# GpSimd out of all operand splits, Silu on ScalarE in half of the heads, and a new order of projections and next weights in a two-block layer stack

## The chip, the core and the metric

The kernel runs on one core of a Trainium2 chip. The metric is the device time of one execution in microseconds (us), the median of several runs. A core has five engines that run side by side, each in its own order: TensorE (PE) multiplies, VectorE (DVE) does elementwise work, ScalarE (ACT) applies functions and copies, GpSimd (POOL) does slower elementwise work and some data movement, SyncE (SP) issues most DMAs. They wait for each other through semaphores.

## The reference, cut to what matters

`reference()` runs 256 tokens of width 1024 through two blocks. The first has a state-space mixer, a stick-breaking attention and two feed-forward layers (FFN, inner width 2816) with RMS norms. The second block has two layers of the form FFN, hybrid mixer, FFN, each followed by a layernorm of residual plus update. The hybrid mixer is what the change is mostly about:

```python
def hybrid_mixer(x, w_in, conv_w, ...):
    hcat = x @ w_in                       # one wide projection, split into:
    qa, ka, va, qkv_b, beta_raw, dt_raw, z, gate_raw = jnp.split(hcat, SPLIT_POINTS, axis=-1)
    ya = sliding_window_attention(qa, ka, va, pos_bias, sink) @ w_branch_a
    qkv_b = jax.nn.silu(causal_depthwise_conv(qkv_b, conv_w))      # width 4, 3072 channels
    qb, kb, vb = jnp.split(qkv_b, (QK_B, 2 * QK_B), axis=-1)
    qb, kb = l2norm(qb), l2norm(kb)       # per head of 128: t * rsqrt(sum(t*t) + 1e-6)
    ...
    o = gated_delta_rule(qb, kb, vb, g, beta)     # chunked recurrence, 8 heads
    yb = (rmsnorm(o) * dn_norm_g * silu(z)) @ w_branch_b
    return (sigmoid(gate_a) * ya + sigmoid(gate_b) * yb) @ w_out
```

## The kernel before, in words

**Operands in two parts.** Matmuls are done in a fast float32 form whose operands are first split: `split` (L151) lets ScalarE copy a tile into the high part `h` (L153), and then the low part is `l = src - h` (L157). Each product is three matmuls (`mm3`: high x low, high x high, low x high). With `share`, the last `share` columns of the subtract are done by GpSimd, the rest by DVE. Only the 48 units of the convolved projections (24 per mixer) use a share, `SH_C = 512` of 1024 columns.

**Weight units.** `unit` (L161) loads 512 KB (128 x 1024) through SP into one of three `raw` buffers and splits it into `wh` and `wl`. The raw buffer is free again when both have read it. `behind_norm` orders a unit's split behind the instructions that stand in `c.norm`: the last ones of a norm, or of the splits of its transposed output.

**Order.** `weave` writes PE's order by hand. It steps through the fill list (projections, one after another) and through lanes (the small chains: heads, windows, prep), which yield how much PE work must pass, or the name of something that has to be done, before they go on. The other engines' order is made by a planner from dependences, priorities and its own estimate of time; a norm with its transposes (`urgent`) has precedence.

**Ends of stages.** `last_rows` (L281) ends a row-wise matmul stage. It keeps the last units' weights and does the first 128 tokens (t = 0) with all of them, starts that half's norm (`tail`), then does t = 1 with its own norm. Before all of that it calls `early`, which loads and splits the first four units of the next stage. The norm's output is transposed on PE, and split (`xx`), 3.9 us of planned PE work after the tail's start; the next stage's products of t = 0 come then, and behind them the transposes of t = 1. There are nine such ends with a next stage: four with an RMS norm, three FFN ends with a layernorm, two ends of `w_out` (five kept units in place of six) with a layernorm.

**The hybrid mixer's projections.** Its fill list is `z_first()`, `betas()`, `conv_half(0)`, `conv_half(1)`, `qkv_a()`, `z_gate(2)`, `z_gate(3)`, the gates, and branch a. `conv_half(f)` does four heads: four keys (n = 1), four queries (n = 0), then four values (n = 2), each a `conv` (L1150): 24 matmuls, then the last tap on ScalarE (L1157), three taps on DVE (L1081, 255, 254 and 253 columns), a Tanh on ScalarE, and a closing product on DVE, `(tanh(a/2) + 1) * a`, twice the silu. `qkv_a` does the windowed attention's two key units, one value unit pair and eight query units, without a convolution. A window lane starts when its query is done.

**prep.** `prep(f)` (L1312) waits until all keys and queries of its half are there, squares them on ScalarE (L1320), sums the squares by four matmuls with `sel` on PE, and goes on to the decay rows, a round trip through DRAM, the Gram matrices of four heads and a small triangular inverse on GpSimd. Heads of that half wait for it.

Of the kernel before, what the change touches and what calls it, by code (L numbers as in the profile page):

```python
# [1 line left out]

# [14 lines left out]
T = 256  # L17
# [74 lines left out]
class Core:  # L92
# [68 lines left out]
    def unit(self, src, share=0, hold=False, stay=False):  # L161
# [11 lines left out]
        with self.behind_norm():  # L173
            self.split(h, l, raw, share)
# [69 lines left out]
    def toks256_steps(self, out, src, x, share=0):  # L244
        ws = [self.unit(src[j], share) for j in range(2)]
        for t in range(2):
            yield from self.toks(out, ws, x, t)
# [45 lines left out]
    def row_gemm(self, units, g, tail, hold=None, wait=lambda j: None, apart=True, share=0):  # L293
# [5 lines left out]
        for j in range(n):  # L299
# [4 lines left out]
            w = self.unit(units[j], share, apart and j >= n - hold)  # L304
# [208 lines left out]
PS = ()  # L513
# [10 lines left out]
def ssm(c, yT, after):  # L524
# [27 lines left out]
    with ExitStack() as ctx:  # L552
# [233 lines left out]
        def group(kt):  # L786
# [94 lines left out]
            c.split(yT[0][:, kt, :], yT[1][:, kt, :], y, 256 if kt in PS else 0)  # L881
# [179 lines left out]
ORD = 2  # L1061
# [8 lines left out]
SH_C = 512  # L1070
# [3 lines left out]
def hybrid(c, i, hT, state, place):  # L1074
# [11 lines left out]
    with ExitStack() as ctx:  # L1086
# [56 lines left out]
        def beta_cols():  # L1143
            for f in range(2):
# [3 lines left out]
                V.tensor_copy(out=bcol[:, f], in_=pt)  # L1148

        def conv(f, n, m):  # L1150

            src = n * NH + m
            w = c.unit(W("qkv")[src], SH_C)
# [26 lines left out]
        def conv_half(f):  # L1180
            heads = range(f * NHH, f * NHH + NHH)
            for n in (1, 0):
                for m in heads:
                    yield from conv(f, n, m)
            c.done.add(f"kq{f}")
            if f == 0:
                beta_cols()
            for m in heads:
                vT[m] = yield from conv(f, 2, m)
                c.done.add(f"vT{m}")  # L1190
# [7 lines left out]
        def qkv_a():  # L1198
            for m in range(2):
                ka[m] = keep1(T)  # L1200
                yield from plain(W("ka")[m], ka[m], 1.0)
# [4 lines left out]
            for m in range(KD):  # L1206
                qa[m] = keep1(T)
                yield from plain(W("qa")[m], qa[m], 0.125)
                c.done.add(f"qa{m}")
# [327 lines left out]

        weave(c,
# [356 lines left out]
```

## Time and profile before

| | |
|---|---|
| median of 3 runs | 2198.07 us (2197.18 to 2202.41) |
| the profiled execution's own time | 2201.57 us |
| its span, first to last instruction | 2199.7 us |
| mean granted TensorE clock | 0.984 of full speed |
| PE busy | 2120.7 us, 96% of the span |
| DVE busy | 1535.2 us, 70% |
| ACT busy | 1181.9 us, 54% |
| POOL busy | 227.4 us, 10%; 77.1 us of it in 48 half subtracts |
| chain that ended last | PE 68%, DVE 11%, DMA 8%, issue 5%, ACT 4%, POOL 2% |

The page gives each engine's busy time, the span in 40 slices, the chain of work that ended last, and groups of instructions by line, tile and shape with their mean duration and the idle time before them. The matmuls are pipelined, so a busy PE may still be late; what tells is how many matmuls a stretch holds, where PE waits and for whom, and where the granted clock is 0.5 (the 1.2 GHz level) instead of 1 (2.4 GHz). The two mixers lie between 906 and 1245 us and between 1642 and 1980 us.

### The profile page before, as it was taken

The numbers are of one execution on the slowest core, as the hardware profiler recorded it, in microseconds if no ns is written. First come the engines' busy times: TensorE is split into PE (matmuls) and PEld (weight loads), VectorE is DVE, ScalarE is ACT, GpSimd is POOL, SyncE is SP. The second block draws the span as 40 slices with busy tenths as digits, with TensorE's granted clock in tenths as the row PEclk, the third lists the DMA queues.
The fourth block names the chain that finished last, engine by engine and source line by source line (L and its number), as shares of the span: only waits on it lengthen the run. The fifth ranks groups of instructions, "written<-read, shape, count | busy, mean of one in ns | idle before, by whom it ended". The sixth has DMA issues, their size and how long they took to land.

```text
span 2199.7 us, 36566 instructions
## 1 busy us (share of the span) xinstructions
PE 2120.7 (96%) x13908; PEld 1855.6 (84%) x13908; DVE 1535.2 (70%) x2615; ACT 1181.9 (54%) x2187; POOL 227.4 (10%) x360
## 2 busy tenths in 40 slices
PE   8799999999999999998999999999999899999998
PEld 7677888898888888887899888888889688998886
DVE  8855777675877666788755776676678876576665
ACT  4644656444655555465655455545546565544553
POOL 1001000000000000342400000000005242000000
PEclk9889999999999999999999999999999999999999
DMA  4315576534666565554433655556555453355663
GB/s 145 104 38 171 184 249 200 174 117 131 199 188 210 174 190 192 169 173 141 140 100 115 219 172 191 185 192 191 189 181 166 138 169 107 103 183 185 193 190 123
DMA packets 123471, 362.02 MB, mean 165 GB/s; under 512 B 24732, under 2 KB 38000, under 8 KB 123296
## 3 DMA queue, kind: packets, MB, share of 16 engines
q1 hardware_dynamic: 117696, 350.25, 51.1%
q0 software_dynamic: 5232, 9.37, 1.5%
q8 instruction: 110, 1.80, 0.3%
q14 instruction: 65, 0.53, 0.1%
q10 hardware_dynamic: 368, 0.07, 0.0%
HBM read 355.36 MB, written 5.04 MB: 164 GB/s over the span
## 4 chain that ended last, share of the span: by engine, by line
PE 68%; DVE 11%; DMA 8%; issue 5%; ACT 4%; POOL 2%; SPq 0%; POOLq 0%; ACTq 0%; DVEq 0%
PE ps L37 65%; DVE wl L157 4%; PE ps L41 3%; ACT wh L153 3%; DMA raw<-in_ffn_w_dram 3%; DVE keep L1081 1%; DVE k L1081 1%; DMA raw<-in_w_out_dram 1%; DMA raw<-in_ffn_w_down_dram 1%; DMA k<-scratch 1%; DMA raw<-in_w_in_z_dram 1%; DMA raw<-in_ssm_w_glu_dram 1%; DMA raw<-in_w_in_qkv_dram 1%; DVE prod L536 1%; POOL u L1080 0%
## 5 line engine op out<-in xcount | busy, mean ns | idle before, releaser
L37 PE MATMUL ps<-xx,wh 128*128 128x256 f32 (+1 forms) x4064 | 1065.5, 337 | 4.9 <-DVE xx L157 2.1
L157 DVE TENSOR_TENSOR wl<-raw,wh 128x1024 fp32r<-128x1024 f32 (+1 forms) x614 | 737.1, 1203 | 321.1 <-ACT wh L153 310.4
L153 ACT CAST wh<-raw 128x1024 fp32r<-128x1024 f32 x614 | 643.4, 1050 | 314.5 <-PE ps L37 157.5
L37 PE MATMUL ps<-xx,wl 128*128 128x256 f32 x2992 | 798.2, 280 | 0.5 <-DVE wl L157 0.5
L37 PEld LDWEIGHTS ps<-xx,wh 128*128 128x128 f32 x4064 | 678.6, 189 | 91.0 <-issue 18.9
L37 PEld LDWEIGHTS ps<-xx,wl 128*128 128x128 f32 x2992 | 563.7, 188 | 21.4 <-DVE wl L157 0.9
L37 PE MATMUL ps<-wh,xx 128*128 128x256 f32 (+1 forms) x1152 | 256.0, 317 | 0.8 <-DVE xx L157 0.7
L230 ACT COPY sum<-ps 128x256 f32<-128x256 f32 x240 | 88.7, 371 | 247.2 <-PE ps L37 246.9
L37 PE MATMUL ps<-wl,gh 128*128 128x512 f32 x528 | 208.9, 396 | 0.0
L37 PE MATMUL ps<-wh,gl 128*128 128x512 f32 x528 | 208.6, 395 | 0.2 <-DVE gl L157 0.2
L37 PE MATMUL ps<-wh,gh 128*128 128x512 f32 x528 | 208.3, 394 | 0.0
L37 PEld LDWEIGHTS ps<-wh,xx 128*128 128x128 f32 x1152 | 190.8, 190 | 17.0 <-DVE xx L157 2.6
L37 PE MATMUL ps<-wl,xx 128*128 128x256 f32 (+1 forms) x576 | 187.7, 326 | 3.8 <-DVE wl L157 3.8
L231 DVE TENSOR_TENSOR sum<-ps,sum 128x256 f32<-128x256 f32 x240 | 101.0, 422 | 108.6 <-ACT sum L230 108.4
L37 PEld LDWEIGHTS ps<-wl,xx 128*128 128x128 f32 x576 | 109.7, 190 | 13.4 <-issue 2.8
L37 PEld LDWEIGHTS ps<-wh,gl 128*128 128x128 f32 x528 | 99.1, 188 | 24.0 <-DVE gl L157 0.9
L37 PEld LDWEIGHTS ps<-wh,gh 128*128 128x128 f32 x528 | 99.3, 188 | 23.3
L37 PEld LDWEIGHTS ps<-wl,gh 128*128 128x128 f32 x528 | 99.2, 188 | 19.1
L337 POOL TENSOR_SCALAR v<-mv 128x1 f32<-128x1 f32 x12 | 7.3, 610 | 846.4 <-DVE mv L394 846.4
L153 ACT CAST xx<-ps 128x512 fp32r<-128x512 f32 (+1 forms) x64 | 31.8, 512 | 107.0 <-PE ps L41 106.5
L157 POOL TENSOR_TENSOR wl<-raw,wh 128x512 fp32r<-128x512 f32 x48 | 77.1, 1613 | 69.6 <-ACT wh L153 64.3
L1081 DVE SCALAR_TENSOR_TENSOR k<-ps,cw,k 128x255 f32<-128x255 f32 x144 | 68.4, 475 | 2.2
(291 smaller groups left out, 2315.0 us busy)
## 6 DMA issues: line engine op xcount, KB each, us to landing
raw<-in_ffn_w_dram SPq DMA_DIRECT2D x264, 512.0 KB, 3.6
raw<-in_ffn_w_up_dram SPq DMA_DIRECT2D x88, 512.0 KB, 3.6
raw<-in_w_in_qkv_dram SPq DMA_DIRECT2D x48, 512.0 KB, 3.7
raw<-in_ffn_w_down_dram SPq DMA_DIRECT2D x44, 512.0 KB, 3.5
raw<-in_w_in_gate_dram SPq DMA_DIRECT2D x32, 512.0 KB, 3.6
raw<-in_w_branch_dram SPq DMA_DIRECT2D x32, 512.0 KB, 3.5
raw<-in_ssm_w_glu_dram SPq DMA_DIRECT2D x16, 512.0 KB, 4.0
raw<-in_w_in_z_dram SPq DMA_DIRECT2D x16, 512.0 KB, 4.3
```

The source lines that it names most:

```text
L37: self.pe.matmul(out, lhsT=lhsT, rhs=rhs, start=start, stop=stop)
L41: self.pe.transpose(out, in_, ident)
L153: o = [self.nc.scalar.copy(out=h, in_=src).ins]
L157: r = e.tensor_tensor(out=l[..., c], in0=src[..., c], in1=h.bitcast(F32)[..., c], op=ALU.subtract)
L230: self.nc.scalar.copy(out=s, in_=ps[:, 1])
L231: self.nc.vector.tensor_tensor(out=s, in0=ps[:, 0], in1=s, op=ALU.add)
L337: nc.gpsimd.tensor_scalar(out=v, in0=ms, scalar1=scale, scalar2=eps, op0=ALU.mult, op1=ALU.add)
L536: e.tensor_tensor(out=o, in0=a, in1=b, op=op)
L1081: stt = lambda o, a, s, b, op0, op1, e=V: e.scalar_tensor_tensor(out=o, in0=a, scalar=s, in1=b, op0=op0, op1=op1)
```

## The change

GpSimd's share goes from every split. `split` gets a flag `behind`, and only the DVE subtract of a unit, no longer ScalarE's copy, is ordered behind `c.norm`. In the first four heads, keys and queries of the convolution take one Silu on ScalarE in place of a Tanh and a product; since they are no longer doubled, the epsilon of their norm changes with them. `prep` waits for one query after another, squares each pair of key and query behind its query, and sums them as they come. The convolutions of the second four heads alternate with the attention's keys, values and queries. And `last_rows` calls `early` after the tail of t = 0 has been started.

```diff
-    def split(self, h, l, src, share=0):
-        o = [self.nc.scalar.copy(out=h, in_=src).ins]
-        n = src.shape[-1] - share
-        for e, c in ((self.nc.vector, slice(0, n)), (self.nc.gpsimd, slice(n, None))):
-            if c.start != src.shape[-1] and c.stop != 0:
-                r = e.tensor_tensor(out=l[..., c], in0=src[..., c], in1=h.bitcast(F32)[..., c], op=ALU.subtract)
-                o.append(r.ins)
-        return o
+    def split(self, h, l, src, behind=False):
+        o = self.nc.scalar.copy(out=h, in_=src)
+        with self.behind_norm() if behind else ExitStack():
+            r = self.nc.vector.tensor_tensor(out=l, in0=src, in1=h.bitcast(F32), op=ALU.subtract)
+        return [o.ins, r.ins]
@@ unit
-        with self.behind_norm():
-            self.split(h, l, raw, share)
+        self.split(h, l, raw, True)
@@ last_rows
-        if self.early:
-            self.early()
-            self.early = None
         for t in range(2):
             for n in range(2):
                 for w, g, first in held:
                     self.rows(acc, w, t, g, first, w is held[-1][0], (n,))
                     yield 1
             self.start(tail(t, acc[2 * t:2 * t + 2]))
+            if self.early:
+                self.early()
+                self.early = None
@@ conv (24 per mixer)
-            w = c.unit(W("qkv")[src], SH_C)
+            w = c.unit(W("qkv")[src])
...
-            h = k1(T)
-            c.act(out=h, in_=a, func=AF.Tanh, scale=0.5)
-            if n == 2:
-                stt(h, h, 1.0, a, ALU.add, ALU.mult)
-                return h
             if n == 1:
                 kq[m] = keep2(2, T)
-            stt(kq[m][:, 1 - n], h, 1.0, a, ALU.add, ALU.mult)
+            if n < 2 and f == 0:
+                c.act(out=kq[m][:, 1 - n], in_=a, func=AF.Silu)
+            else:
+                h = k1(T)
+                c.act(out=h, in_=a, func=AF.Tanh, scale=0.5)
+                stt(h if n == 2 else kq[m][:, 1 - n], h, 1.0, a, ALU.add, ALU.mult)
+            if n == 0:
+                c.done.add(f"q{m}")
+            if n == 2:
+                vT[m] = h
+                c.done.add(f"vT{m}")
@@ prep
-            yield f"kq{f}"
-            pss = c.ps(2, T)
-            sq = []
+            pss = None
             for h in range(NHH):
-                sq.append(k2(2, T))
-                S.activation(out=sq[h], in_=kq[f * NHH + h], func=AF.Square)
-            yield hop()
-            for h in range(NHH):
-                PE.matmul(pss[:NHH], lhsT=sel[:, h, :], rhs=sq[h], start=h == 0, stop=h == NHH - 1)
-                yield 0.4
+                yield f"q{f * NHH + h}"
+                yield hop()
+                sq = k2(2, T)
+                S.activation(out=sq, in_=kq[f * NHH + h], func=AF.Square)
+                yield hop()
+                if h == 0:
+                    pss = c.ps(2, T)
+                PE.matmul(pss[:NHH], lhsT=sel[:, h, :], rhs=sq, start=h == 0, stop=h == NHH - 1)
+            yield 0.8
             lr = k2(2, T, part=NHH)
-            V.tensor_scalar(out=lr, in0=pss[:NHH], scalar1=4e-6, scalar2=None, op0=ALU.add)
+            V.tensor_scalar(out=lr, in0=pss[:NHH], scalar1=(EPS, 4 * EPS)[f], scalar2=None, op0=ALU.add)
@@ the mixer's fill list
+        (kq0, v0), (kq1, v1) = conv_half(0), conv_half(1)
+        light = [keys_a(0), keys_a(1), values_a()] + [queries(m) for m in range(KD)]
+        mixed = [g for pair in zip_longest(kq1 + v1, light) for g in pair if g]
...
-               2: [z_first(), betas(), conv_half(0), conv_half(1), qkv_a(), z_gate(2), z_gate(3),
-               gates(0, ca), gates(1, gb), branch_a()],
+              [z_first(), betas(), *kq0, beta_cols(), *v0, *mixed, z_gate(2), z_gate(3), gates(0, ca), gates(1, gb),
+               branch_a()])
@@ attention to FFN (first block)
-        def early():
-            ho.append(c.pair(1))
-            ho.extend(up_ahead(ho[0], 1))
-            c.early()
         def to_ffn(t, acc):
+            if t == 0:
+                ho.append(c.pair(1))
+                ho.extend(up_ahead(ho[0], 1))
             yield from to_norm(ho[0], g)(t, c.add(t, acc))
```

## Rows read from the trace of the kernel before

**Rows 1.** The page, first part: busy us, share of the span, instructions.
```profile
PE 2120.7 (96%) x13908; PEld 1855.6 (84%) x13908; DVE 1535.2 (70%) x2615; ACT 1181.9 (54%) x2187; POOL 227.4 (10%) x360
```
**Rows 2.** Stretches: length, busy us (instructions) of PE, PEld, DVE, ACT, POOL; clock; DMA.
```profile
925.00:950.00 25.00, 25.00 (x216) 24.85 (x215) 22.11 (x39) 17.41 (x31) 13.85 (x11) 1.00 0.66 208
1000.00:1025.00 25.00, 19.50 (x112) 13.98 (x111) 21.74 (x53) 14.61 (x28) 0.00 (x0) 0.86 0.26 90
1250.00:1275.00 25.00, 21.05 (x108) 17.86 (x107) 16.40 (x24) 4.32 (x5) 3.38 (x4) 0.86 0.55 184
1725.00:1750.00 25.00, 16.98 (x93) 11.76 (x92) 20.77 (x46) 13.20 (x27) 5.19 (x3) 0.86 0.42 130
```
**Rows 3.** PE's waits, whole span: us in total, times, longest us.
```profile
PE ps L37 <- ACT k L1320: 11.7, 7, 4.5
PE ps L41 <- DVE x L399: 11.2, 5, 4.2
```
**Rows 4.** PE's waits from 975 to 1025 us, the same columns.
```profile
PE ps L37 <- ACT k L1320: 5.5, 3, 4.5
PE ps L37 <- DVE keep L1080: 1.1, 1, 1.1
```
**Rows 5.** DVE's groups by shape, whole span: busy us, mean ns, idle before.
```profile
L157 DVE TENSOR_TENSOR wl<-raw,wh 128x1024 fp32r<-128x1024 f32 x566 | 692.4, 1225 | 313.8 <-ACT wh L153 303.4 <-PE ps L41 1.3
...
L157 DVE TENSOR_TENSOR wl<-raw,wh 128x512 fp32r<-128x512 f32 x48 | 44.9, 935 | 7.2 <-ACT wh L153 6.9
L157 DVE TENSOR_TENSOR xx<-ps,xx 128x512 fp32r<-128x512 f32 x40 | 27.2, 688 | 26.6 <-ACT xx L153 26.6
L1081 DVE SCALAR_TENSOR_TENSOR keep<-k,k 128x256 f32<-128x256 f32 x32 | 24.3, 760 | 4.3 <-ACT k L279 4.2
...
L1081 DVE SCALAR_TENSOR_TENSOR k<-k,k 128x256 f32<-128x256 f32 x16 | 10.0, 625 | 2.7 <-ACT k L279 2.7
```
**Rows 6.** DVE in order of time, convolutions: start, us, line, operation, tiles, shape.
```profile
935.06 1.53 DVE L1081 SCALAR_TENSOR_TENSOR keep<-k,k 128x256 f32<-128x256 f32 x1
...
939.19 0.41 DVE L1081 SCALAR_TENSOR_TENSOR keep<-k,k 128x256 f32<-128x256 f32 x1
```
**Rows 7.** ACT's groups by shape from 922 to 1000 us.
```profile
L279 ACT ACT_TABLE_LOAD x2 | 2.6, 1283 | 0.0
```
**Rows 8.** ACT's groups by shape, whole span: the FFN's Silu.
```profile
L415 ACT ACTIVATE s<-sum 128x256 f32<-128x256 f32 x80 | 33.4, 417 | 1.3 <-DVE sum L231 1.2
```
**Rows 9.** PE in order of time, first w_out end; idle before in brackets.
```profile
1259.32 0.39 PE L37 MATMUL ps<-wl,xx 128*128 128x512 f32 x1
1259.55 0.62 PE L37 MATMUL ps<-wh,xx 128*128 128x512 f32 x2
1264.11 1.11 PE L41 MATMUL ps<-ident,x 128*128 128x128 f32 x4 [3.94 <-DVE x L399]
```
**Rows 10.** DVE in order of time at the same place.
```profile
1257.36 2.48 DVE L157 TENSOR_TENSOR wl<-raw,wh 128x1024 fp32r<-128x1024 f32 x2 [1.69 <-ACT wh L153]
1259.75 0.69 DVE L391 SCALAR_TENSOR_TENSOR xn<-ps,x 128x512 f32<-128x512 f32 x1
1260.47 0.69 DVE L392 BATCH_NORM_STATS2 st<-xn 128x6 f32<-128x512 f32 x1
...
1263.30 0.75 DVE L399 SCALAR_TENSOR_TENSOR x<-xn,r,gain 128x512 f32<-128x512 f32 x1 [0.45 <-POOL r L339]
```
**Rows 11.** DVE in order of time, an FFN's end.
```profile
1449.06 0.67 DVE L391 SCALAR_TENSOR_TENSOR xn<-ps,x 128x512 f32<-128x512 f32 x1
...
1452.10 1.40 DVE L399 SCALAR_TENSOR_TENSOR x<-xn,r,gain 128x512 f32<-128x512 f32 x2
```
**Rows 12.** PE at the same FFN's end, second transposes.
```profile
1462.34 0.60 PE L41 MATMUL ps<-ident,x 128*128 128x128 f32 x4
```
**Rows 13.** The page, DMA issues: queue, count, KB each, us to landing.
```profile
raw<-in_ffn_w_dram SPq DMA_DIRECT2D x264, 512.0 KB, 3.6
```

More of the change, by code (lines that the diff above doesn't have):

```diff
@@ L1 @@
 from contextlib import ExitStack
+from itertools import zip_longest
 import numpy as np
@@ L148, in norm_pools, with unit @@
         self.gain = self.pool(ctx, "gain", 2)
-    def split(self, h, l, src, share=0):
-        o = [self.nc.scalar.copy(out=h, in_=src).ins]
-        n = src.shape[-1] - share
-        for e, c in ((self.nc.vector, slice(0, n)), (self.nc.gpsimd, slice(n, None))):
-            if c.start != src.shape[-1] and c.stop != 0:
-                r = e.tensor_tensor(out=l[..., c], in0=src[..., c], in1=h.bitcast(F32)[..., c], op=ALU.subtract)
-                o.append(r.ins)
-        return o
-    def unit(self, src, share=0, hold=False, stay=False):
+    def split(self, h, l, src, behind=False):
[3 more added lines that the diff above has]
+        return [o.ins, r.ins]
+    def unit(self, src, hold=False, stay=False):
         raw = (self.hold_raw if hold else self.raw).tile([P, 1024], F32, name="raw")
@@ L242, in toks, with toks256_steps @@
                 yield 1
-    def toks256_steps(self, out, src, x, share=0):
-        ws = [self.unit(src[j], share) for j in range(2)]
+    def toks256_steps(self, out, src, x):
+        ws = [self.unit(src[j]) for j in range(2)]
         for t in range(2):
@@ L291, in last_rows, with row_gemm @@
             self.start(tail(t, acc[2 * t:2 * t + 2]))
-    def row_gemm(self, units, g, tail, hold=None, wait=lambda j: None, apart=True, share=0):
+            if self.early:
+                self.early()
+                self.early = None
+    def row_gemm(self, units, g, tail, hold=None, wait=lambda j: None, apart=True):
         n, held, acc, hold = units.shape[0], [], None, hold or HOLD
@@ L303, in row_gemm @@
                 acc = [self.ps() for _ in range(4)]
-            w = self.unit(units[j], share, apart and j >= n - hold)
+            w = self.unit(units[j], apart and j >= n - hold)
             if j < n - hold:
@@ L512 @@
 NR = 2
-PS = ()
 TURNS = {0: (0,), 1: (1,), 3: (2,), 5: (3,)}
@@ L880, in group @@
             S.activation(out=y, in_=y, func=AF.Gelu_apprx_tanh)
-            c.split(yT[0][:, kt, :], yT[1][:, kt, :], y, 256 if kt in PS else 0)
+            c.split(yT[0][:, kt, :], yT[1][:, kt, :], y)
             c.done.add(f"y{kt}")
@@ L1060 @@
 QQ = (2, 2)
-ORD = 2
 VF = 14.0
@@ L1069 @@
 LW = 2
-SH_C = 512
 HOP = 2.4
@@ L1148, in beta_cols @@
                 V.tensor_copy(out=bcol[:, f], in_=pt)
+            yield 0
         def conv(f, n, m):
             src = n * NH + m
-            w = c.unit(W("qkv")[src], SH_C)
+            w = c.unit(W("qkv")[src])
             p = c.ps(T)
@@ L1181, in conv_half @@
             heads = range(f * NHH, f * NHH + NHH)
[L1182 to L1190, printed above, removed]
+            return [conv(f, n, m) for n in (1, 0) for m in heads], [conv(f, 2, m) for m in heads]
         def plain(src, dst, scale):
@@ L1196, in plain, with queries, keys_a, values_a @@
             S.activation(out=dst, in_=p, func=AF.Copy, scale=scale)
[L1198 to L1201, printed above, removed]
+        def queries(m):
+            qa[m] = keep1(T)
+            yield from plain(W("qa")[m], qa[m], 0.125)
+            c.done.add(f"qa{m}")
+        def keys_a(m):
+            ka[m] = keep1(T)
+            yield from plain(W("ka")[m], ka[m], 1.0)
+        def values_a():
             p = c.ps(2, T)
@@ L1205, in qkv_a @@
             S.copy(out=ka["v"], in_=p)
[L1206 to L1209, printed above, removed]
         def z_first():
@@ L1543, in hybrid @@
                ] + [[window(j) for j in range(n, KD, LW)] for n in range(LW)],
-              {0: [z_first(), betas(), conv_half(0), qkv_a(), conv_half(1), z_gate(2), z_gate(3),
-               gates(0, ca), gates(1, gb), branch_a()],
-               1: [betas(), conv_half(0), z_first(), conv_half(1), qkv_a(), z_gate(2), z_gate(3),
-               gates(0, ca), gates(1, gb), branch_a()],
-               2: [z_first(), betas(), conv_half(0), conv_half(1), qkv_a(), z_gate(2), z_gate(3),
-               gates(0, ca), gates(1, gb), branch_a()],
-               3: [z_first(), betas(), conv_half(0), z_gate(2), z_gate(3), conv_half(1), qkv_a(),
-               gates(0, ca), gates(1, gb), branch_a()],
-               4: [z_first(), betas(), conv_half(0), gates(0, ca), conv_half(1), qkv_a(), z_gate(2), z_gate(3),
-               gates(1, gb), branch_a()]}[ORD])
+              [z_first(), betas(), *kq0, beta_cols(), *v0, *mixed, z_gate(2), z_gate(3), gates(0, ca), gates(1, gb),
+               branch_a()])
         cT = c.pair(place)
@@ L1743, in first_block @@
         out = c.row_gemm(I["attn_w_o"], c.ktiles(oT), to_ffn, 4, wait=lambda j: f"o{max(j, 5)}")
-        c.early = early
         stick_breaking(c, hk, state, 1, c.gains(I["norm_mix"][1]), oT, [out, go()])
```

## The prediction

> **What bounds the kernel now.** I read the busy shares, then TensorE (PE) in stretches, then PE's waits, and then the engine that each wait names. PE is busy for 96% of the span, so time is to be won only where PE stands still or runs on the slow clock [rows 1]. In the dense stretch 925:950 PE issues 216 matmuls; in 1000:1025 it issues 112, in 1725:1750 only 93, and in both the granted clock is 0.86, that is some 7 us at the 1.2 GHz level (0.14 x 25 x 2) [rows 2]. Both are the same place of the two hybrid mixers: the projections with the causal convolution are just over. Of all PE's waits the longest are on the squares of prep (11.7 us) and on the layernorm's output (11.2 us) [rows 3]. The squares are waited for because VectorE (DVE) is behind: it is busy 22.1 of 25 us in the convolutions, against 25 us of a PE that never stops there [rows 2], and the ScalarE squares can't start before DVE's last product of the convolution.
>
> **Why DVE is behind.** In the 48 convolution units GpSimd subtracts columns 512 to 1023. That leaves DVE 935 ns for its half; a whole 1024 columns takes 1225 ns [rows 5]. And the closing product takes 1.53 us in one unit and 0.41 us in a later one [rows 6]; its mean is 760 ns for q and k (32 of them) and 625 ns for v (16) [rows 5]. In the slow one a GpSimd subtract runs beside it. So the half given away saves DVE little and costs it elsewhere.
>
> **Part 1, split and silu.** DVE loses 44.9 us of half subtracts and gains 48 x 1.225 = 58.8 us. Of the 32 products of q and k, 16 become one Silu on ScalarE: 16 x 0.76 = 12.2 us less. The other 16 and the 16 of v fall to 0.41 us: 16 x 0.35 + 16 x 0.215 = 9.0 us less. Sum: -7.3 us of DVE, 3.7 per mixer. On ScalarE a Silu of this shape takes 417 ns [rows 8] and replaces a Tanh of the same shape; the Silu's own function table adds two loads per mixer (in, and back to Tanh and Exp), 4 x 1.28 = 5.1 us [rows 7], beside 7.6 us of idle ScalarE in 25 us [rows 2]: I cost them at nothing; if that cover failed, +5.1.
>
> **Part 2, the order.** So far 24 convolution units stand in a row. Now 12 do, and the other 12 alternate with 11 plain units (attention queries, keys, values), each of which asks DVE only for the 1.2 us subtract. DVE per convolution unit was 0.94 + three taps + 0.76; it is now 1.23 + three taps + 0.41 or 0, and the second half of the units is spread over twice the PE time. What this can remove: the 11.7 us of waits on squares, 1.1 us of a neighbouring wait in each mixer of which I take half [rows 4], and the slow clock that follows the stop. PE works through about 4.8 of those 7 us and loses half of that, 2.4 per mixer. Sum: 11.7 + 1.1 + 4.8 = 17.6 us.
> What comes back: the squares now follow each query and may not be late by more than two hops of PE work. In the second half they fall into prep(0)'s own DVE work, and the window lanes, whose queries come earlier, bring theirs into the same stretch. The nearest row for such a wait is the one removed, 4.5 us [rows 4], with its clock 6.9; the bounds are 0 and 6.9 per mixer. I take the middle, 3 for each, since DVE has less work in more PE time, but not by much. Net of parts 1 and 2: -11.6 us, with bounds -17.6 and -3.8. prep(1) also comes eight units later; prep(0)'s heads fill the lanes meanwhile, and after them follow gates and branch matmuls, so I cost that at nothing; without this cover it is 8 x 2.8 = 22 us.
>
> **Part 3, next weights behind the norm.** There are nine places where a stage ends and the next one's four first weights are split. At the end of each mixer (w_out) DVE does two of these subtracts, 2.48 us, having stood idle for their copy, and only then takes the norm's second half at 1259.75 [rows 10]. PE's accumulation for it was ready 21 matmuls before the transposes: 21 x 0.23 us before 1259.8 is 1255.0 [rows 9]. From that start to the first half of x pass 4.3 us (1259.75 to 1264.05) [rows 10], so x would be ready at 1259.6, just when PE wants it. That takes away 3.9 and 4.2 us of waiting [rows 3, 9], and up to 4.5 us of slow clock (2.8 here [rows 2]; 1.7 at the other, my estimate from half of this dip's length): -12.6. At the three ends of an FFN before a layernorm the waits are 11.2 - 8.1 = 3.1 us in all [rows 3]: -3.1.
> Against that stands DVE's work between the first norm's end and the second norm's x: four subtracts 4.9, two splits of the transposed half 1.4, the second norm's first half 1.4 and its rest 4.3: 12.0 us [rows 5, 10]. In an FFN end the first norm would end at 1453.5 less 1.6 = 1451.9 [rows 11], and the second transposes are due at 1462.3 less 0.6 = 1461.7 [rows 12]: 9.8 us, a shortage of 2.2, three times: +6.6. In a w_out end, which has six matmuls (1.4 us) fewer and where the first norm's end stands nearer to the transposes, I estimate 7.9 us, a shortage of 4.1, twice: +8.2. Before, these subtracts lay under the rows of the first half. The four ends with an RMS norm have shorter DVE work; bounds 0 and 2.2, I take 0.5: +2.0. Net of part 3: -15.7 + 16.8 = +1.1, bounds -15.7 and +23.6 (+2.2 at four ends, 4.1 at two, 2.2 at three, with no wait gone).
> ScalarE's copies are no longer held behind the norm; they are ready before it, and cost nothing unless one that waits for its load (3.6 us [rows 13]) stands ahead of the norm's own casts.
>
> **Sum.** -11.6 + 1.1 = -10.5 us. Against the profiled execution, 2201.6 us (span 2199.7), that is 2191; it lies 3.5 us above the median of the runs, 2198.07, so 2187.6. The shortages of part 3 are counted with no overlap, and DVE can use the idle time in front of the second norm for some of it; I take 1.6 us off: 2186.
>
> **Rivals.**
> *Full relief.* DVE keeps up everywhere and the subtracts find gaps: -17.6 - 12.6 - 3.1 = -33, some 2165. For it: the span of DVE work falls while PE's time stays. Against it: DVE is at 22 of 25 us now [rows 2], and 3.7 us per mixer is little.
> *DVE still full.* The wait moves from prep(1)'s first square to its four squares or to the next subtract: parts 1 and 2 bring 4, part 3 brings -1 to +2: 2194 to 2198, no change. For it: DVE's own sum falls by 7.3 us only. Against it: the plain units that now lie between.
> *The norm's price (other side).* The four subtracts stand as a block ahead of the splits of the transposed half at all nine ends, so the whole 4.9 us is PE's wait: 9 x 4.9 = 44 less 11.6, 12.6 and 3.1 is +17: 2215, slower. It decides from 27.3 / 9 = 3.0 us per end. For it: 12.0 us of work in 7.9 to 9.8. Against it: the tail's work has precedence, and the lag is only the shortage.
> *Function tables.* If Silu and Tanh or Exp alternate, each of 8 Silus per mixer costs two loads of 1.28 [rows 7], 20.5 us against 22 x 0.3 = 6.7 us of ScalarE idle in the 8 units: +14 per mixer, 2214. Against it: the Silus stand in one run of units. The Trainium skill (page "ScalarE: Activation LUTs", section "Table sets: the hidden batching unit") says to batch activations by table set, which speaks against this edit. By its section "What ACT_TABLE_LOAD costs" a switch is 2.66 us with the drain; the two switches per mixer would then be 10.6 us in all, while the trace shows 1.28 for the load.
>
> **How the numbers follow.** Forecast 0.50, full relief 0.18, DVE still full 0.16, norm's price 0.13, tables 0.03. What can be told from no change is 0.3%, 6.6 us, so faster means under 2191.5: the forecast and full relief, 0.68. Between: 0.17, nearly all of DVE still full. Slower: 0.15. The range from 2166 to 2200 takes in full relief's near side and all of DVE still full, and leaves out the norm's price and the tables.
>
> **What would show it.** Right: GpSimd without wl groups; the closing product near 0.41 us; PE's wait on the squares under 6 us in all; no dip of the clock at the end of the convolutions; PE's wait on the layernorm's x at the two w_out ends under 2 us; two more table loads per mixer. Part 3 is wrong if PE waits at the second transposes or on wl by over 3 us at most of the ends. The prediction fails if convolution stretches keep under 180 matmuls in 25 us with DVE full, or if the ends lose more than the mixers gain.

## The result: 1.1% slower, and the profile after

The changed kernel takes 2227.16 us (median of four, 2226.22 to 2227.89), the kernel before 2200.08 in the same series: the ratio is 1.0107, 95% interval 1.0088 to 1.0126. I had forecast 2186, faster. The profiled execution of the changed kernel took 2227.42 us with a span of 2225.6.

First the page's busy times of the changed kernel (busy us, share of the span, instructions), to be held against [rows 1]:

```profile
PE 2135.7 (96%) x13908; PEld 1869.0 (84%) x13908; DVE 1522.4 (68%) x2599; ACT 1186.2 (53%) x2189; POOL 148.9 (7%) x312
```

DVE is busy for 12.8 us less than before, GpSimd for 78.5 us less with 48 instructions fewer, and the span is 25.9 us longer. So the work went where the change sends it, and the loss lies in when it is done and at which clock. The stretches of the changed kernel, as in [rows 2] (the last two are shifted by what the kernel had lost until then):

```profile
925.00:950.00 25.00, 25.00 (x215) 25.00 (x214) 20.36 (x30) 18.94 (x32) 1.53 (x3) 1.00 0.73 224
1000.00:1025.00 25.00, 19.63 (x96) 14.56 (x95) 19.09 (x55) 14.73 (x41) 0.00 (x0) 0.80 0.34 114
1025.00:1050.00 25.00, 22.14 (x156) 18.64 (x156) 16.27 (x43) 12.13 (x28) 12.40 (x32) 0.93 0.40 126
1075.00:1100.00 25.00, 22.38 (x166) 18.57 (x165) 22.65 (x68) 17.54 (x59) 0.00 (x0) 0.93 0.31 101
1225.00:1250.00 25.00, 21.75 (x167) 21.00 (x166) 14.88 (x25) 9.64 (x18) 0.88 (x2) 0.93 0.36 118
1275.00:1300.00 25.00, 21.39 (x149) 19.18 (x148) 20.21 (x25) 8.73 (x12) 5.26 (x5) 1.00 0.55 172
1750.00:1775.00 25.00, 21.05 (x119) 16.97 (x117) 19.60 (x67) 16.60 (x51) 0.00 (x0) 0.86 0.29 93
```

In 925:950 DVE has come down from 22.1 to 20.4 us, as intended. In 1000:1025 PE issues 96 matmuls where it issued 112, and the granted clock is 0.80, that is 10 us at the 1.2 GHz level (0.20 x 25 x 2) instead of 7. The next three stretches also belong to the first mixer and have 0.93 each, where the kernel before has 1.00. In 1275:1300, the end of that mixer, the clock is now 1.00 instead of 0.86. In the second mixer three stretches have 0.86 (1750:1775, 1775:1800, 1975:2000), where the kernel before has one. By these rows PE is at the 1.2 GHz level for some 41 us within the two mixers, branch b included, against 14 before. A matmul of the sums below that takes 592 ns in most cases takes up to 1061 there, so about half of that time is lost, and up to 14 us of the 25.9 are clock (an estimate from these rows, with PE busy throughout).

PE's waits in the changed kernel over the whole span (us in total, times, longest us), as in [rows 3]:

```profile
PE ps L38 <- ACT k L1314: 14.0, 6, 3.9
PE ps L38 <- DVE xx L156: 12.1, 10, 2.8
...
PE ps L42 <- DVE x L396: 6.9, 5, 2.3
```

The wait on the squares (L1314, L1320 before) was to go and has grown from 11.7 to 14.0 us. The wait on the layernorm's x has fallen from 11.2 to 6.9, and the splits of the transposed half (xx), 3.6 us before, cost 12.1. DVE's groups of the changed kernel (busy us, mean ns), as in [rows 5]:

```profile
L156 DVE TENSOR_TENSOR wl<-raw,wh 128x1024 fp32r<-128x1024 f32 x614 | 750.7, 1226 | 317.9 <-ACT wh L154 309.0
...
L1075 DVE SCALAR_TENSOR_TENSOR keep<-k,k 128x256 f32<-128x256 f32 x16 | 7.0, 436 | 4.6 <-ACT k L276 4.6
...
L1075 DVE SCALAR_TENSOR_TENSOR k<-k,k 128x256 f32<-128x256 f32 x16 | 6.7, 421 | 0.1
```

The closing product takes 436 and 421 ns where it took 760 and 625. The Trainium skill states on the page "SBUF — State Buffer", section "Who interferes with whom", that a VectorE instruction with two SBUF inputs contends with a GpSimd instruction that reads SBUF. The traces agree: beside a GpSimd subtract the product took up to 1.53 us [rows 6], and in e4 below, where only GpSimd's share is taken away, it takes 0.41 to 0.43 for the first mixer's queries and keys.

**Where the 25.9 us are.** I cut both executions at the transposes of each normalized output, and the mixers once more at branch b and at w_out:

| piece (us) | before | after | difference |
|---|---|---|---|
| mixer 1, mixer 2: transposes to first projection | 16.9, 16.9 | 19.8, 18.4 | +2.9, +1.5 |
| mixer 1, mixer 2: projections until branch b | 294.6, 294.5 | 304.4, 301.7 | +9.8, +7.2 |
| mixer 1, mixer 2: branch b | 22.4, 22.4 | 24.0, 24.6 | +1.6, +2.2 |
| mixer 1, mixer 2: w_out to the transposes | 24.5, 24.8 | 20.4, 20.4 | -4.1, -4.4 |
| attention end to the next FFN end | 185.5 | 190.0 | +4.5 |
| last stage | 199.9 | 203.5 | +3.6 |
| all others together (the largest: -2.9 and +3.4) | | | +1.1 |

The mixers' projections with what hangs on them lose 20.8 us where I had forecast -11.6; the other pieces lose about 5 on balance where I had +1.1 for the ends of the stages.

**Why the projections lose: the sums of squares stand in series.** The TensorE matmuls that sum the squares (k,sel; eight for each half of the heads) of prep(0) in the first mixer, first in the kernel before and then in the changed kernel (durations, first and last start):

```profile
L37 PE MATMUL ps<-k,sel x8: 592/592/593, 953.4 to 961.8; 128*4 128x512 f32 x8
```

```profile
L38 PE MATMUL ps<-k,sel x8: 592/592/592, 954.1 to 980.0; 128*4 128x512 f32 x8
```

They start together and end 18 us apart. Here it isn't the squares that are late. This is the ScalarE group of the four squares of prep(0) in the changed kernel:

```profile
L1314 ACT ACTIVATE k<-keep x4: 631/632/632, 953.4 to 960.9; 128x512 f32<-128x512 f32 x4
```

The last square is done at 961.5, and its sum stands on PE at 979.6: PE didn't wait for it, the sum has 18 us of other matmuls ahead of it in PE's own order. Each head's lane has one hop before its square and one before its sum, and the next head's begin only then, so eight hops are in series where there was one. For prep(1) the same rows are, before and after:

```profile
L37 PE MATMUL ps<-k,sel x8: 592/592/1057, 1005.2 to 1016.2; 128*4 128x512 f32 x8
```

```profile
L38 PE MATMUL ps<-k,sel x8: 592/804/1061, 1013.5 to 1053.4; 128*4 128x512 f32 x8
```

So the second half of the heads gets its gates 37 us later (the mixer itself starts 3.5 us later), and here PE does wait. The sum of the first head's squares no longer stands behind all four queries but two hops behind its own, whose convolution DVE has not finished. PE's waits on the squares of prep(1) in the first mixer, from 975 to 1060 us, against 5.5 before [rows 4]:

```profile
PE ps L38 <- ACT k L1314: 6.7, 2, 3.9
```

These are stops of 3.9 and 2.9 us at 1009 and 1030, and the clocks of 0.80 and 0.93 above lie around them: some 13 us at the lower level in place of 7. The second mixer has 6.8 us of such waits and 0.86 in two stretches, some 14 us.

The other part stands at the mixer's end. In the kernel before, in order of time, the last head's transposes, and the first matmul of branch b, with some 40 fill matmuls (xx) between them, so that the head is at most 4.8 us early:

```profile
1212.34 0.38 PE L41 MATMUL ps<-ident,k 128*128 128x128 f32 x2
...
1217.15 0.39 PE L37 MATMUL ps<-keep,wh 128*128 128x256 f32 x2
```

In the changed kernel the fill list is empty at 1227.7 and only the last head's chain is left; in brackets what PE waited:

```profile
1227.65 0.28 PE L38 MATMUL ps<-xx,wl 128*128 128x256 f32 x1
...
1230.40 0.49 PE L38 MATMUL ps<-k,keep 128*128 128x128 f32 x2 [1.05 <-DVE k L1074]
1233.05 0.59 PE L42 MATMUL ps<-ident,k 128*128 128x128 f32 x2 [2.15 <-DVE k L1075]
1233.39 0.49 PE L38 MATMUL ps<-keep,wh 128*128 128x256 f32 x2
```

PE stands still for 3.2 of 5.6 us, and the clock in 1225:1250 is 0.93 (3.5 us at the lower level; before, it was 1.00 around branch b). Together that is about 5 of the 11.4 us which projections and branch b of the first mixer lose. The rest is in the middle: the waits on squares and the clock around them, and the dip in 1075:1100.

**What the norm's edit did.** The w_out end of the first mixer in the changed kernel, DVE in order of time, and below it PE's transposes:

```profile
1276.76 0.75 DVE L396 SCALAR_TENSOR_TENSOR x<-xn,r,gain 128x512 f32<-128x512 f32 x1 [0.45 <-POOL r L336]
1277.42 0.68 DVE L388 SCALAR_TENSOR_TENSOR xn<-ps,x 128x512 f32<-128x512 f32 x1
1278.03 0.74 DVE L396 SCALAR_TENSOR_TENSOR x<-xn,r,gain 128x512 f32<-128x512 f32 x1
1278.68 3.49 DVE L156 TENSOR_TENSOR wl<-raw,wh 128x1024 fp32r<-128x1024 f32 x3
```

```profile
1277.88 0.60 PE L42 MATMUL ps<-ident,x 128*128 128x128 f32 x4
...
1279.70 0.60 PE L42 MATMUL ps<-ident,x 128*128 128x128 f32 x4
```

No bracket stands at the transposes: the wait of [rows 9] is gone. But three subtracts of weights, 3.5 us, now stand on DVE right behind the norm, ahead of the split of the transposed half, and PE waits 2.2 us for that at 1281. That belongs to the xx group of the waits above. The transposes of t = 1 then wait again:

```profile
1289.36 0.66 PE L42 MATMUL ps<-ident,x 128*128 128x128 f32 x4 [0.96 <-DVE x L396]
```

With some 0.4 us of smaller ones PE waits 3.6 us at this end, behind the place where I cut the table; the kernel before has no wait there. At the second w_out end it waits 4.7 us there. So the table's -4.1 and -4.4 are not net gains: the pieces that follow are 1.0 and 3.6 us longer.

### The profile page after: what moved, and what is told of

The parts are those of the page before. It is cut to its first block, busy times and chain, and to the rows that moved or that the text cites. A ratio compares the mean times of both kernels' runs of the same rounds, so it can differ in the third digit from the quotient of the medians.

```text
span 2225.6 us, 36418 instructions
## 1 busy us (share of the span) xinstructions
PE 2135.7 (96%) x13908; PEld 1869.0 (84%) x13908; DVE 1522.4 (68%) x2599; ACT 1186.2 (53%) x2189; POOL 148.9 (7%) x312
## 4 chain that ended last, share of the span: by engine, by line
PE 80%; DVE 9%; DMA 3%; ACT 3%; issue 2%; POOL 1%; POOLq 0%; DVEq 0%; ACTq 0%; SPq 0%
PE ps L38 77%; DVE wl L156 3%; PE ps L42 2%; DMA raw<-in_ffn_w_dram 1%; DMA k<-scratch 1%; ACT wh L154 1%; DVE k L1074 1%; ACT k L276 1%; DVE k L1075 1%; DVE prod L532 1%; POOL r L336 0%; POOL v L334 0%; DVE xn L375 0%; DVE xn L388 0%; ACT L276 0%
## 5 line engine op out<-in xcount | busy, mean ns | idle before, releaser
L156 DVE TENSOR_TENSOR wl<-raw,wh 128x1024 fp32r<-128x1024 f32 x614 | 750.7, 1226 | 317.9 <-ACT wh L154 309.0
L38 PEld LDWEIGHTS ps<-wh,xx 128*128 128x128 f32 x1152 | 192.4, 192 | 26.7 <-DVE xx L156 12.8
L156 DVE TENSOR_TENSOR xx<-ps,xx 128x512 fp32r<-128x512 f32 (+1 forms) x64 | 36.2, 586 | 33.3 <-ACT xx L154 33.3
```

The costliest lines, as they stand in the source:

```text
L38: self.pe.matmul(out, lhsT=lhsT, rhs=rhs, start=start, stop=stop)
L156: r = self.nc.vector.tensor_tensor(out=l, in0=src, in1=h.bitcast(F32), op=ALU.subtract)
```

## The experiments

Medians are given with the ratio to the kernel before on the same chip (2201.3 to 2203.0 us) and its 95% interval. Differences between two experiments are of medians; they come from several chips, and where the intervals of two ratios overlap I say so. "After" is the changed kernel; the first experiments undo one part of it.

### e1_early_first: the weights of the next stage ahead of the last rows again

```diff
+        if self.early:
+            self.early()
+            self.early = None
         for t in range(2):
             ...
             self.start(tail(t, acc[2 * t:2 * t + 2]))
-            if self.early: ...
... (and the attention's end calls its `early` as before)
```

> The changed kernel, with the next weights' loads and splits called ahead of the last rows again, as before. Theory (three separate losses: squares in series make the heads late; the ends of the stages; waits on squares that stay): by the trace, the ends of the stages cost the changed kernel 6 to 7 us net (losses of 3 to 5 us at four ends, gains of 4 us at each w_out end), so this is 2220 us (2215 to 2224), the w_out transposes wait about 4 us again and the wait for xx splits (12.1 us in ten places) falls under 5. Rival (the new place of the weights is the main loss, over 20 us): 2205 or less. Rival (it is a net gain because of w_out): 2230 or more.

Measured 2216.19 us, 1.0069 (1.0048 to 1.0091): 11 us faster than after. The wait on x is back at 11.3 us, that on xx falls from 12.1 to 2.5. So part 3 by itself costs 11 us on balance, more than the 5 of the table.

### e2_squares_at_once: prep waits for its last query, squares all four, sums all four

```diff
-            for h in range(NHH):
-                yield f"q{f * NHH + h}"
-                yield hop()
-                (square of head h)
-                yield hop()
-                (sum of head h)
+            yield f"q{f * NHH + NHH - 1}"
+            (four squares)
+            yield hop()
+            (four sums, 0.4 apart)
```

> The changed kernel, with the squares of prep made together after the last query of the half, one hop, then the four sums, as before. Theory: the two hops per head in series end prep(0)'s sums at 979.6 instead of 961.4 us (before), this makes the heads end behind the fill list, and costs 7 to 9 us per mixer; undone, prep(0)'s sums end about 15 us earlier, PE has no stop between branch a and branch b, and the time is 2211 us (2206 to 2217). Rival (the alternating order makes the second half's heads late, whatever prep(0) does): 2224 or more, the stop at the end of the mixer stays.

Measured 2201.31 us, 0.9997 (0.9983 to 1.0010): the whole loss of 26 us is gone with this one edit, where I had expected 16. The projections take 290.7 and 289.6 us instead of 304.4 and 301.7 (in the profiled execution, at 2195.84 us the fastest of ten). The sums of prep(1) in this kernel:

```profile
L38 PE MATMUL ps<-k,sel x8: 592/592/593, 1029.4 to 1037.8; 128*4 128x512 f32 x8
```

They end 16 us sooner than after, though still 21 later than before. PE's waits of this kernel from 985 to 1240 us:

```profile
PE ps L42 <- DVE k L1075: 2.4, 1, 2.4
...
PE ps L38 <- ACT k L1314: 0.9, 1, 0.9
```

The first is the last head's chain, which still ends behind the fill list: the stop that I expected to go is 2.4 us, and 0.3 ahead of it, where it was 3.2. What is gone is the waits on squares, 0.9 us in place of 6.7, and the slow clock. The stretches of the same matmuls, and the mixer's end:

```profile
1000.00:1025.00 25.00, 24.30 (x184) 22.34 (x185) 22.73 (x67) 13.60 (x33) 1.33 (x2) 1.00 0.54 166
1025.00:1050.00 25.00, 23.94 (x162) 18.51 (x161) 18.50 (x45) 16.10 (x32) 13.54 (x36) 1.00 0.44 125
1210.00:1235.00 25.00, 22.35 (x188) 21.94 (x187) 16.00 (x28) 11.01 (x18) 1.02 (x2) 1.00 0.44 142
```

No 25 us stretch of either mixer is below 1.00 in this execution. Over all executions the mean clock is 0.983 to 0.989 in e2 and 0.979 to 0.981 in the changed kernel. So what the edit wins lies more at the squares than at the mixer's end.

### e8_behind_no_hops: squares behind each query, without the hops of each head

```diff
             for h in range(NHH):
                 yield f"q{f * NHH + h}"
-                yield hop()
                 (square of head h)
-                yield hop()
-                (sum of head h)
+            yield hop()
+            (four sums, 0.4 apart)
```

> The changed kernel with each square still made behind its query, but without the two hops per head: the four squares are issued as the queries come, then one hop, then the four sums together. Theory (the series of hops is what makes prep(0) late, not that squares follow queries): as e2, 2201 us (2197 to 2206), no stop at the end of the mixer. Rival (squares spread among the convolutions delay ScalarE and DVE): 2212 or more.

Measured 2202.39 us, 1.0008 (0.9995 to 1.0022), the same as e2. Squares behind their queries do no harm; the hops in series do, in this order of the fill list. The stop at the mixer's end is 2.4 us here too, against my expectation.

### e12_series_first_half: the hops in series for prep(0) alone

```diff
+            if f: (prep(1): four squares after its last query, a hop, four sums)
+            else: (prep(0): as in the changed kernel)
```

> The changed kernel with squares in series for the first half of the heads alone; prep(1) makes them at once, as in e2. Theory (what decides is when prep(1)'s sums end: before 1016, e3 1033, e2 1038 us without a stop at the end of the mixer, the changed kernel 1053 with one; e3 has prep(0) as late as the changed kernel and loses nothing by it): near e2, 2203 us (2199 to 2209), no stop before branch b. Rival (prep(0)'s lateness is what makes the heads late): 2220 or more, with the stop.

Measured 2209.07 us, 1.0030 (1.0012 to 1.0048): just above the range that I expected. Of the 26 us, 18 come back with prep(1)'s series gone, and 8 stay with prep(0)'s. The sums of prep(1) end at 1039.8, two us later than in e2, and PE waits 0.3 us on the squares. So prep(0)'s series isn't free, as the theory had it, and the time at which prep(1)'s sums end does not decide alone. The stop before branch b, which was to be gone, is 2.4 us as in e2, but with a lower clock around it:

```profile
1210.00:1235.00 25.00, 22.57 (x181) 21.97 (x179) 13.97 (x25) 9.78 (x20) 1.96 (x4) 0.93 0.37 126
```

The projections take 296.0 and 295.8 us against 290.7 and 289.6, by profiled executions that are 15 us apart; I can't place the 8 us more closely.

### e3_not_mixed: the old order of the fill list, everything else as after

```diff
-        mixed = [g for pair in zip_longest(kq1 + v1, light) for g in pair if g]
+        mixed = kq1 + v1 + light
```

> The changed kernel, with the fill list in the old order: all 24 convolutions, then the eleven attention units. Theory: the squares in series of prep(0) are unchanged, so heads 0 to 2 stay late, but prep(1) is ready some 20 us earlier; the windows come later and lie beside the heads again; the stop at the end of the mixer shrinks from 5 to 2 us, the waits on squares stay at 10 us or more: 2222 us (2216 to 2230). Rival (the order is the main loss): 2212 or less, no stop at the end of the mixer.

Measured 2194.70 us, 0.9962 (0.9949 to 0.9975): 32 us faster than after, 27 more than I expected. prep(0)'s sums still end late, at 982.3, but prep(1)'s queries come sooner and its sums end at 1032.7. No stop is left at the mixer's end; of the waits over 0.1 us from 985 to 1240 one is left:

```profile
PE ps L38 <- ACT k L1314: 5.7, 1, 5.7
```

So the mixed order pushes prep(1) back too. The two repairs work at different places: this one takes away the stop at the mixer's end and keeps 5.7 us of wait on a square, e2 takes away the waits on squares and keeps a stop of 2.4 us.

### e5_at_once_not_mixed: both repairs together

```diff
-            (prep in series, as in the changed kernel)
+            (prep at once, as in e2)
-        mixed = [g for pair in zip_longest(kq1 + v1, light) for g in pair if g]
+        mixed = kq1 + v1 + light
```

> The changed kernel with both undone: squares at once (as in e2) and the fill list in the old order (as in e3). Both runs took away the same stop at the end of the mixer. Theory (one loss, two ways to remove it: heads that end behind the fill list): the gains don't add, the heads end early either way; the waits on prep(1)'s squares stay as in e3, 12 us: 2194 us (2189 to 2199). Rival (two losses that add, 26 and 32 us): 2180 or less.

Measured 2213.47 us, 1.0054 (1.0034 to 1.0074): worse than either repair alone, by 12 and 19 us, and against every expectation. prep(1)'s sums end at 1022.5 and nothing waits at the mixer's end. The loss is in the convolutions; PE's waits from 985 to 1240 us:

```profile
PE ps L38 <- ACT k L1314: 5.5, 2, 4.4
PE ps L42 <- DVE k L1075: 5.1, 1, 5.1
PE ps L38 <- ACT keep L1188: 4.3, 1, 4.3
```

Three stops of 4 to 5 us stand at 989, 1007 and 1046, each for work that is behind on DVE or ScalarE, and the clock is 0.86 in 980:1005 and in 1005:1030. So the series of hops, which costs 26 us in the mixed order, is worth 19 us in the old one. With the convolution units in a row again and prep at once, prep's own DVE work falls among them. That the series helps e3 by spreading that work is my reading; no run isolates it.

### e4_share_out: the kernel before, with only GpSimd's half of the splits given to DVE

```diff
-SH_C = 512
+SH_C = 0
```

> The kernel before, with nothing changed but GpSimd's share of the 48 convolution splits, which DVE does too. Theory: a whole subtract costs DVE 1.23 us in place of 0.94 and the closing products fall from 0.76 and 0.63 to 0.41 us, DVE's sum is nearly the same (+14 - 14 us), the squares of prep(1) are waited for as before: 2198 us (2194 to 2202). Rival (DVE can't take the whole subtract; this is where the change loses): 2210 or more, with PE waiting on wl. Rival (the shared work of GpSimd is what makes DVE late): 2190 or less, the 4.5 us wait on the first square under 2.

Measured 2209.12 us, 1.0032 (1.0019 to 1.0046): 8 us slower, where I expected 3 faster. The mixer's first 97 us, in the kernel before and in e4 (columns as in [rows 2]):

```profile
922.60:1020.00 97.40, 88.25 (x647) 76.94 (x646) 84.94 (x162) 59.02 (x111) 40.43 (x30) 0.96 0.50 158
```

```profile
922.60:1020.00 97.40, 84.98 (x615) 74.57 (x614) 78.07 (x150) 56.07 (x102) 3.28 (x6) 0.95 0.51 157
```

DVE's busy time falls by 6.9 us, and PE issues 32 matmuls fewer. What DVE waited for in that stretch, in the kernel before and in e4:

```profile
DVE wl L157 <- ACT wh L153: 5.1, 9, 1.5
```

```profile
DVE wl L157 <- ACT wh L153: 9.7, 13, 2.0
```

My reading is that DVE works in order: while a whole subtract waits for its copy on ScalarE, the product behind it waits too, and then PE for that. PE's waits on DVE's L1081 in this stretch are 4.7 and 2.2 us, where the kernel before has none over 0.7. No run isolates it.

### e6_tanh: e2 with Tanh and a product for all heads

```diff
-            if n < 2 and f == 0:
+            if False:
```

The factor 2 that the products then leave in q and k goes into prep's epsilon, 4 * EPS for both halves, as it was before the change.

> As e2, but with Tanh and a closing product in all heads, no Silu. Theory: DVE has 16 more products of 0.42 us, 3.4 us per mixer, in a stage where PE now waits little for DVE, and ScalarE two loads of its function table fewer per mixer; Silu is worth 0 to 4 us: 2203 us (2200 to 2208). Rival (the table loads stand in the chain to the squares): 2198 or less. Rival (Silu is what keeps DVE up): 2210 or more.

Measured 2212.08 us, 1.0053 (1.0038 to 1.0069): the Silu of four heads is worth 10.8 us by the two medians (12 by the two ratios), where I had expected 2. Without it PE waits for the squares again (us over the whole span, 1.8 in e2), in the first mixer mostly for those of prep(0), whose heads had the Silu:

```profile
PE ps L38 <- ACT k L1314: 9.9, 5, 3.3
```

### e7_behind_at_wout: e2 with the weights behind the norm only at the two w_out ends

```diff
+        if self.early and not self.after_norm:
+            self.early()
+            self.early = None
         for t in range(2): ...
+                c.after_norm = True     (around the mixers' w_out alone)
```

> As e2, but the next weights are called behind the norm at the two ends of w_out alone, and ahead of the last rows at the seven other ends, as before. Theory: at the seven ends the subtracts between the two norms cost 3.6 us (state-space end), 4.1 us (attention end) and about nothing at the FFN ends, at w_out the four or so per end stay won: 2194 us (2190 to 2198), waits for xx splits fall from 11.9 to 7 us. Rival (the ends are even, as forecast): 2200 or more.

(The attention's end has its `early` as before; the same holds for e9 to e11.) Measured 2197.25 us, 0.9984 (0.9966 to 1.0001): 4.1 us under e2 by the medians, but the intervals overlap. The wait on xx falls from 11.9 to 7.1.

### e9_not_mixed_wout: e3 with the placement of e7

```diff
-        mixed = [g for pair in zip_longest(kq1 + v1, light) for g in pair if g]
+        mixed = kq1 + v1 + light
+        if self.early and not self.after_norm: (the weights, as before the change)
```

> The changed kernel with the old fill order (as e3) and the next weights behind the norm at w_out alone (as e7). Theory (the two are independent: e3 is 32 us under the changed kernel, the place of the weights brought e7 4 us over e2): 2190 us (2186 to 2195), beats before and the changed kernel; the start of the mixers is 16.9 us long as before, not 18 to 20, and the w_out end 20.4. Rival (they collide, since the mixers then start earlier against the same loads): 2196 or more.

Measured 2182.02 us, 0.9908 (0.9890 to 0.9925): faster than both kernels, by 20 us and 45 us, and faster than I expected. Against e3, which differs only in the place of the weights at seven ends, it is 12.7 us faster, with intervals that lie apart. Whether the two w_out ends are better with the weights behind the norm than without was not run. The page's busy times:

```profile
PE 2113.3 (97%) x13908; PEld 1856.9 (85%) x13908; DVE 1527.3 (70%) x2599; ACT 1185.3 (54%) x2189; POOL 148.5 (7%) x312
```

PE has the same instructions as after in 22 us less of busy time. The projections take 288.9 and 286.6 us, and prep(1)'s sums end at 1020.7.

### e10_silu_all: e9 with Silu for all eight heads

```diff
-            if n < 2 and f == 0:
+            if n < 2:
... (and prep's epsilon is EPS for both halves)
```

> As e9, with Silu for queries and keys of all eight heads. Theory (the first square of prep(1) waits 5.7 us because its query's convolution is late on DVE; a product of 0.42 us less in eight more units brings it forward): the wait on squares falls from 12 to under 7 us, and the time is 3 to 8 us under e9: 2185 us (2180 to 2190). Rival (ScalarE's function tables now alternate, Silu against Tanh, Ln and Exp of prep(0) and the values: more than 14 loads per mixer): 2195 or more.

Measured 2185.66 us, 0.9924 (0.9908 to 0.9939): in the range, but only because e9 came out faster than thought. It is not faster than e9, and the two intervals overlap. The wait on squares is 9.4 us, where I expected under 7. ScalarE's table loads in e9 and in e10 at the line of all activations:

```profile
L277 ACT ACT_TABLE_LOAD x12 | 15.4, 1283 | 0.9 <-DVE k L1079 0.3 <-issue 0.3
```

```profile
L277 ACT ACT_TABLE_LOAD x22 | 28.2, 1283 | 11.7 <-DMA k<-scratch 8.6 <-DVE k L1079 2.5 <-issue 0.3
```

In the second half the Silus stand among other activations, and the set is switched five more times per mixer. The Trainium skill (page "ScalarE: Activation LUTs", section "Table sets: the hidden batching unit") has the rule that activations of one set should be done together. In the first half, where the Silus stand together, the traces have one load more per mixer (12 in all, 10 in the kernel before and in e6), and the Silu gains 10.8 us with that load (e6).

### e11_share_back: e9 with GpSimd's half of the convolution splits back

```diff
-            w = c.unit(W("qkv")[src])
+            w = c.unit(W("qkv")[src], share=512)
```

The split again gives its last 512 columns to GpSimd.

> As e9, with GpSimd's half of the convolution splits given back. Theory from e4 (taking the share away cost the kernel before 8 us, because DVE, which works in order, then stands longer in each subtract while others wait behind it): faster than e9 by 3 to 8 us, 2185 us (2181 to 2189). Rival (e4's loss was a matter of one wait in the old order; with Silu the closing products that GpSimd slows down are what counts): slower than e9 by 2 us or more.

Measured 2182.17 us, 0.9902 (0.9881 to 0.9924): no difference from e9 that these runs can tell, so neither the theory nor the rival holds. The edit that my prediction began with, GpSimd out of the splits, costs 8 us in the old kernel and nothing that can be told in the best one.

## Why the prediction was wrong, step by step

**The step that failed** is in part 2, in the two terms for what comes back. First, "the squares now follow each query and may not be late by more than two hops": the diff has two hops in each of four heads, one after the other, and each sum now stands on PE's path by itself. I priced what comes back at 3 us per mixer, between 0 and 6.9. In the first mixer PE waited 7.0 us for squares, with some 13 us at the lower clock around it, of which about 6 are lost (an estimate from the rows): 13 us, above my upper bound, and as much in the second. Second, "prep(1) also comes eight units later; prep(0)'s heads fill the lanes meanwhile, and after them follow gates and branch matmuls, so I cost that at nothing": prep(1)'s sums end 37 us later, and the mixer's end pays about 5 us for that, with the fill list empty. I had named the cover and priced its absence at 22 us; what I did not do was measure it. In the trace of before the last head ended 4.8 us ahead of branch b.

What is shown by experiment: without the series the whole 26 us are gone (e2), also with the squares behind their queries (e8), and prep(1)'s share is 18 of them (e12). Shown as well: the series costs this only together with the mixed order (e3, e5). That most of it lies at the squares and their clock, not at the mixer's end, is read from the traces: e2 and e8 keep a stop of 2.4 us there.

**DVE's relief** was right as work and wrong as time. The closing product fell to the forecast 0.41 us nearly, and DVE's busy time by 12.8 us where I had -7.3. (The subtracts and closing products alone give -7.2, as forecast.) I took the busy share, 22.1 of 25 us, for the reason of DVE's lateness. But in e4 DVE is less busy and the kernel is slower, and e11 and e9 differ neither in DVE's busy time (1527.1 and 1527.3 us) nor in the time of the kernel. The Silu, of which I counted only the 12.2 us of products, is the edit of part 1 that paid: 10.8 us. It also takes DVE's product out of the chain from convolution to square; which of the two pays was not tested.

**The squares.** Forecast: 11.7 us of waits go and 3 per mixer come back. In fact 14.0 stand there. In e2 only 1.8 are left, so the removal was to be had. There the projections take 3.9 and 4.9 us less than before, together 8.8 where I had 11.6, though in an execution 5.5 us under e2's median.

**Part 3** was right at its first place: the waits of 3.9 and 4.2 us on x ahead of the transposes are gone (-4.1 and -4.4 by the table; I had -12.6 with all of the clock, part of which lay in the next stage). But waits of 3.6 and 4.7 us behind the transposes take their place. The payback was put at the right instruction, DVE's split of the transposed half behind the weights' subtracts, and PE's waits there grow by 8.5 us, from 3.6 to 12.1. What was mis-sized is the gain of 15.7: the waits on x fall by 4.3 us and not by 11.2. Undoing part 3 wins 11 us (e1) where I had +1.1; the rest of these 11 I can't place. The rival "the norm's price" wanted 4.9 us at every end and didn't come.

**Tables:** one load more per mixer, not two. No run has the Silu without its load, so its price alone isn't shown.

**The forecast's other signs:** GpSimd lost its 48 subtracts, right; squares under 6 us, wrong; no dip of the clock behind the convolutions, wrong (0.80 for 0.86); PE's wait on x at w_out under 2 us, right.

**Open:** why e5 is slower than e2 and e3, beyond the place of its three stops and the clock there; what prep(0)'s series costs in detail in e12; and whether the weights behind the norm pay at the w_out ends.

## What to carry to other kernels

When an edit puts waits or hops into a lane, count them in series over all heads, and ask of each matmul that moves forward whether what it reads is ready there; a matmul that waits holds up all that stands behind it in PE's order. Hold the delay at the lane's end against the slack that the last lane has; here 4.8 us of slack met 37 us of delay. The busy share of an engine that works in order is not its lateness: look at the chain in front of the late instruction (e4, e6). A prefetch behind a norm moves waits as well as removing them, so judge it end by end, with the stage that follows (e9 against e3: 12.7 us for taking it back at seven of nine ends).

## What the runs showed of the hardware

A stop of 2.4 us at the mixer's end went with a granted clock of 1.00 around it in e2 and with 0.93 in e12. In the changed kernel the two stops of 1.05 and 2.15 us there, with little work between, had 0.93 around them, and 1000:1025, with a stop of 1.5 us at 1000 and one of 3.9 us at 1009, had 0.80. What a stop costs is not its length alone. And ScalarE had the last square of prep(0) done 18 us ahead of the matmul that reads it: an engine's own order, not the data, can be what makes a result late.
